# Conformer convolution stage on one core: TensorE convolves a feature tile behind the next tile's projection, and the shifted copy that it reads is made in two parts

## The chip, the cores and the metric

The kernel runs on one core of a Trainium2 chip. The metric is the device time of one execution in microseconds (us); lower is better. A core has TensorE (PE, matrix products into PSUM; PEld are its weight loads), VectorE (DVE), ScalarE (ACT), GpSimd (POOL), and SyncE (SP), which issues nearly all DMA transfers of this kernel. Each engine works through its own list of instructions in order; semaphores tie the lists together.

## What is computed

One inference step of an encoder with two layers, for 512 frames of a new stream and 16 frames each of 8 running streams: 640 frames of 1024 features. Layer 0 is a convolution module and an FFN, layer 1 attends to shared keys and values and has an FFN too. The change lies in the convolution module, which is:

```python
def conv_module(h, hist, g, w_pw1, b_pw1, w_dw, b_dw, ln_g, ln_b, w_pw2, b_pw2):
    a, gate = jnp.split(rms_norm(h, g) @ w_pw1 + b_pw1, 2, axis=-1)
    glu = a * jax.nn.sigmoid(gate)
    full = jnp.concatenate([hist, glu], axis=1)        # 30 earlier frames in front
    y = depthwise_conv(full, w_dw) + b_dw              # width 31, each feature by itself
    y = jax.nn.silu(layer_norm(y, ln_g, ln_b))         # mean and variance over the 1024 features
    return h + y @ w_pw2 + b_pw2, full[:, -30:]
```

Everything is float32. A dense product is done as three products of float32r halves (weight high by input high, weight low by input high, weight high by input low), so one output tile of 128 features by 320 frames with 1024 inputs takes 8 x 3 = 24 matmuls.

## The kernel before

Features lie on partitions: the 1024 features are 8 tiles of 128, called c0 to c7 here. The 640 frames are two halves g = 0 and 1 of 320 columns; half 0 holds the 128 sample frames and the first 192 prompt frames, half 1 the other 320 prompt frames.

The module is a list of steps, the string `PLAN`, which `step` works off one by one. Within what the steps issue, a scheduler then sets the order on each engine from priorities and its own timing (`high_priority` blocks are moved ahead); so the order that stands in the program is read off the built program. The steps:

- `a`, `b`, `c`: the projection of a tile, `glu`. It makes four PSUM tiles (two halves of frames, each with a value and a gate; 24 matmuls each), one after the other. ACT reads each out (L563 the tanh of the gate, L566 the value), DVE multiplies them into the buffer `gall` (L570 the sample frames, L576 the prompt frames). The weights of a tile come with `wsplit`: a DMA into `raw`, ACT makes the high half `whi` (L139), DVE the low half `wlo` (L143). All three have two buffers. PSUM has four buffers of the tag `mm`, which projections and convolutions share.
- `d`: the convolution of a tile on DVE (`conv`, L604: 31 multiply-adds per piece, the sum in PSUM). This is how the sample part of c0 to c3 and the prompt part of c1 and c2 are done.
- `q`: the prompt part of c0 and c3 on ACT and POOL (`conv_pool`): ACT makes a product of 512 columns for each tap (L614, tile `cvt`, two buffers), POOL adds it to a sum `ca` (L617). ACT copies the finished sum to `y` (L583).
- `l`, then `S`, `A`, `B`: c4 to c7 on TensorE. `conv_load` has POOL build diagonal weights `w4` (L622) and copies the tile's row of `gall` to DRAM (`sc`, L627); `conv_shift` reads it back in four DMAs, shifted by 0 to 3 frames, into `x4` (L633). `conv_pe` then does 32 matmuls of 32 output rows for each part (L647): `S` the sample frames (128 columns), `A` the prompt frames of half 0 (192), `B` those of half 1 (320). ACT adds the bias and writes `y` (L583).
- `n0`, `n1`: the layer norm of a half (`conv_ln`): `colmean` sums the features by matmuls with a column of constants (L194, three for each tile), after adding the first `LCUT` = 6 tiles up on POOL (L185); `spread` sends a result back to all partitions (L206); squares on ACT (L166); POOL takes the power (L233); DVE multiplies, ACT takes the silu and the high halves.
- `w0`, `w1`: the second projection `pw2` of a half, and after it the FFN.

The string, with `l4 A4 S4 B4` right behind the projection `c4`:

```python
PLAN = ("a0 y a1 x b0 b1 q0 dp1s0 c2 ds1p2 c3 q3 ds2s3 c4 l4 A4 S4 B4 c5 l5 A5 S5 B5 "
        "c6 l6 A6 S6 c7 l7 A7 S7 s0 n0 B6 B7 w0 n1 w1")
```

`x` is the RMS norm of half 1, `s0` writes the convolution history out (`out_convs`, 1472 KB, and `out_convp`).

Of the kernel before, what the change touches and what calls it, by code (L numbers as in the profile page):

```python
# [15 lines left out]
P = 128  # L16
# [31 lines left out]
C01 = 4  # L48
NB1 = 2
SSQ = 'avavavav'  # L50
SCUT = 8
# [17 lines left out]
def tile_trunk(ctx, tc, xT, vecs, hist, w_pw1, w_pw2, w_in0, w_out0, w_in1, w_out1,  # L69
# [9 lines left out]
    uid = [0]  # L79
    gr = list(GS)  # L80
    mm = tps.enter_context(tc.tile_pool(name="mm0", bufs=4, space=PSUM))
    tp = tps.enter_context(tc.tile_pool(name="tp0", bufs=2))
# [80 lines left out]
    def square(s, n, eng="a"):  # L163
        q = tp.tile([P, 384], F32, tag="sq", name=nm("sq"))
# [9 lines left out]

    def colmean(st, pieces, n, cut, tag, eng=nc.gpsimd):
        nt = len(tiles(n))
        srcs = []
        prev = acc = None
        for s in pieces[:cut]:
            if prev is None:  # L180
                prev = s()
                continue
            if acc is None:
                acc = tp.tile([P, 384], F32, tag="acc", name=nm("acc"), bufs=1)
            eng.tensor_tensor(out=acc[:, :n], in0=prev, in1=s(), op=ALU.add)  # L185
            prev = acc[:, :n]
        if prev is not None:
            srcs.append(lambda: prev)
        srcs += pieces[cut:]
        w = len(srcs)  # L190
        for k, f in enumerate(srcs):
            s = f()
            for t, a in enumerate(tiles(n)):
                nc.tensor.matmul(st[:, 512 + t * w + k:513 + t * w + k], s[:, a:a + P],  # L194
                                 onec, start=True, stop=True)
# [24 lines left out]

    def rstd_bc(pieces, n, engs=SQ, cut=CUT, r2=None, eng=nc.gpsimd, newton=False):
        st = w2t()
        nt = len(tiles(n))
        r, v = colmean(st, [lambda s=s, e=e: square(s, n, e) for s, e in zip(pieces, engs)], n,
                       cut, "rst", eng)
        nc.vector.tensor_scalar(out=r[:, :nt], in0=v, scalar1=EPS, scalar2=None,
                                op0=ALU.add)
        if r2 is None:
            r2 = tp.tile([P, 4], F32, tag="rst2", name=nm("rst2"))
        if newton:  # L230
            rsqrt(r2[:, :nt], r[:, :nt])
        else:
            nc.gpsimd.tensor_tensor(out=r2[:, :nt], in0=r[:, :nt], in1=mhalf[:, :nt], op=ALU.pow)  # L233
        return spread(st, r2, n), r2
# [4 lines left out]

    def rms(g, gain, engs=SQ, cut=CUT, eng=nc.gpsimd):  # L240
        n = gr[g][1]
        bc, _ = rstd_bc([hp(g, k) for k in range(KT)], n, engs, cut, None, eng)
        xh, xl = new_xs(g)
        for k in range(KT):
            t = tp.tile([P, 384], F32, tag="n1", name=nm("n1"), bufs=NB1)
            nc.vector.scalar_tensor_tensor(out=t[:, :n], in0=hp(g, k), scalar=col(gain, k),
                                           in1=bc, op0=ALU.mult, op1=ALU.mult)
            xsplit(t[:, :n], xh[:, k, :], xl[:, k, :])
        return xh, xl, None, None

    def rms_late(g, gain, engs=SQ, cut=CUT):
        n = gr[g][1]
        xh, xl = new_xs(g)
        for k in range(KT):
            src = hp(g, k)
            if gain is not None:
                t = tp.tile([P, 384], F32, tag="n1", name=nm("n1"), bufs=NB1)
# [293 lines left out]

    def glu(c, g, wh, wl):
        n = gr[g][1]
        ps = []
        for ab in range(2):
# [3 lines left out]
                xk(xs[g], range(KT)))  # L559
            ps.append(pt[:, :n])  # L560
        with tc.high_priority(offset=HP):
            t = tp.tile([P, 384], F32, tag="t1", name=nm("t1"))
            nc.scalar.activation(out=t[:, :n], in_=ps[1], func=AF.Tanh, scale=0.5,  # L563
                                 bias=hb1[:, KT + c:KT + c + 1])
            a = tp.tile([P, 384], F32, tag="t2", name=nm("t2"))
            nc.scalar.activation(out=a[:, :n], in_=ps[0], func=AF.Identity, scale=0.5,  # L566
# [42 lines left out]
    def conv_pool(c):  # L609
        acc = cp.tile([P, T], F32, tag="ca", name=nm("ca"))  # L610
        for j in range(W):
            wj = dcol(V_DW + c * W + j)
            pr = acc if j == 0 else cp.tile([P, T], F32, tag="cvt", name=nm("cvt"), bufs=2)
            nc.scalar.activation(out=pr, in_=taps(c, 1, j), func=AF.Identity, scale=wj,  # L614
                                 **({} if j else {"bias": col(V_BDW, c)}))
            if j:
                nc.gpsimd.tensor_tensor(out=acc, in0=acc, in1=pr, op=ALU.add)  # L617
        to_y(c, NB * SB, T, acc, func=AF.Copy)

    def conv_load(c):  # L620
        w4 = cp.tile([P, 32, 32], F32, tag="w4", name=nm("w4"), bufs=2)
        nc.gpsimd.tensor_tensor(  # L622
            out=w4, in0=i4[:, None, :].to_broadcast([P, 32, 32]),
            in1=dwv[:, V_DW4 + 32 * c:V_DW4 + 32 * c + 32].unsqueeze(2).to_broadcast([P, 32, 32]),
            op=ALU.mult)
# [4 lines left out]
    def conv_shift(sc, n):  # L630
        x4 = cp.tile([P, 4, NSC + NPC - 4], F32, tag="x4", name=nm("x4"), bufs=2)
# [5 lines left out]
    def conv_pe(c, w4, x4, a, n):  # L637
        pt = mmt()
        for tg in range(8):
            for q in range(4):  # L640
                if a < 0:
                    mv = x4[:, q, 0:NSC].rearrange("p (s w) -> p s w", w=SEG)
                    mv = mv[:, :, 4 * tg:4 * tg + SB]
                else:
                    o = NSC + a + 4 * tg
                    mv = x4[:, q, o:o + n]
                nc.tensor.matmul(pt[32 * q:32 * q + 32, 0:n], w4[:, 4 * tg + q, :], mv,  # L647
                                 start=(tg == 0), stop=(tg == 7))
        to_y(c, 0 if a < 0 else NB * SB + a, n, pt, func=AF.Identity, bias=col(V_BDW, c))

    def conv_ln(g):
        n = gr[g][1]
        mu = w2t()
        order = LNO[g]
        r, v = colmean(mu, [lambda c=c: y[g][:, c, :] for c in order], n, LCUT, "mst")
        if v is not r:
# [7 lines left out]
        for c in range(KT):  # L664
            yc = y[g][:, c, :]
            nc.vector.tensor_tensor(out=yc, in0=yc, in1=bc, op=ALU.mult)
            s = tp.tile([P, 384], F32, tag="n1", name=nm("n1"), bufs=NB1)
            nc.scalar.activation(out=s[:, :n], in_=yc, func=AF.Silu, scale=col(V_LNG, c),
# [4 lines left out]
    def pw2(g, z):  # L673
        n = gr[g][1]
        for m2 in range(KT // 2):
            wh, wl = wsplit(w_pw2[m2], 16, P, pool=PL2[g])
            for i in range(2):
# [10 lines left out]
    def step(op, arg):  # L688
# [5 lines left out]
        elif op == "c":  # L694
            w = wsplit(w_pw1[c], 16, P, pool=PL1[c])
            load_hist(c, c + 1)
# [4 lines left out]
        elif op == "x":  # L701
            xs[1] = rms(1, V_NCONV, SSQ1, 8)
        elif op in "lm":
            w4, sc = conv_load(c)
            x4s[c] = w4, conv_shift(sc, NSC if op == "m" else NSC + NPC - 4)
        elif op == "d":
            conv([(int(arg[i + 1]), int(arg[i] == "p")) for i in range(0, len(arg), 2)])
        elif op == "q":
            conv_pool(c)
        elif op == "S":  # L710
            conv_pe(c, *x4s[c], -1, NB * SB)
        elif op in "pAB":
            a, n = {"p": (0, T), "A": (0, NH - NB * SB), "B": (NH - NB * SB, NH)}[op]
            conv_pe(c, *x4s[c], a, n)
        elif op == "s":
# [12 lines left out]
    hf.close()  # L728
    gr[:] = GR
    tps, early = ExitStack(), ExitStack()  # L730
    op_ = early.enter_context(tc.tile_pool(name="op", bufs=1, reuse_waits="tile"))
# [433 lines left out]
```

## Time and profile before

| | us |
|---|---|
| median of 3 runs | 1636.82 |
| lowest and highest | 1635.42, 1638.98 |
| the profiled execution | 1640.0 |
| its span in the profile | 1638.2 |
| TensorE busy in the span | 1508.8 (92%) |
| start of c5's projection on TensorE, from the span's start | 128.55 |
| first matmul of `pw2`, from the span's start | 277.51 |

A row of a timeline or of the chain gives the start and the length in us, then engine, line, operation, and output <- input; in square brackets stands how long the engine was idle before the row and what ended that. A row of windows gives, for one stretch of time, the busy time of PE, PEld, DVE, ACT and POOL with the number of instructions, the granted TensorE clock as a share of full speed, the DMA share, and GB/s. A row of groups gives all instructions of one kind and shape: number, busy us in total, mean ns of one, then idle time ahead and what ended it. "PE 5956..." in the page is the busy share in tenths in 40 slices of 41 us.

### The profile page before, as it was taken

What the parts mean: (1) busy time and instruction counts of PE and PEld (TensorE: products, weight loads), DVE (VectorE), ACT (ScalarE), POOL (GpSimd) and SP (SyncE); (2) the same over time, 40 slices, a digit from 0 to 9 for tenths busy, and PEclk for the clock granted to TensorE, in tenths of its full rate; (3) what the DMA queues carried; (4) which work ended last, traced back from release to release, by engine and by line L of the source; (5) the groups of instructions that cost most, each with busy time, mean ns of one, the idle gap of its engine ahead of it and who ended that gap; (6) DMA issues with size and microseconds to landing.
All of it is one profiled execution on the core that took longest, in us unless ns stands there. A gap on an engine that the chain in (4) does not pass through costs nothing.

```text
span 1638.2 us, 27200 instructions
## 1 busy us (share of the span) xinstructions
PE 1508.8 (92%) x11156; PEld 1435.8 (88%) x11156; DVE 996.3 (61%) x1990; ACT 675.5 (41%) x1295; POOL 244.6 (15%) x259
## 2 busy tenths in 40 slices
PE   5956659999999999999899899997899999999997
PEld 5955558989999999999898689895899999999997
DVE  5798003479557557556566656765486565566655
ACT  3565114445424325334555435453344244244243
POOL 5588200410000000001422211110100000000001
PEclk9977776999999999999999999999899999999998
DMA  6243340331222312312445545553012222223211
GB/s 212 71 115 84 83 123 1 103 129 46 84 78 71 110 52 81 100 63 92 139 145 183 174 139 181 171 186 116 26 52 79 102 78 68 87 78 104 78 52 64
DMA packets 52891, 163.99 MB, mean 100 GB/s; under 512 B 9632, under 2 KB 21536, under 8 KB 44064
## 3 DMA queue, kind: packets, MB, share of 16 engines
q1 hardware_dynamic: 52480, 161.96, 30.7%
q8 instruction: 87, 1.43, 0.4%
q10 hardware_dynamic: 288, 0.31, 0.1%
q14 instruction: 36, 0.29, 0.1%
HBM read 150.89 MB, written 11.36 MB: 99 GB/s over the span
## 4 chain that ended last, share of the span: by engine, by line
PE 83%; DVE 5%; POOL 5%; DMA 4%; ACT 2%; issue 2%; SPq 0%; POOLq 0%; DVEq 0%; ACTq 0%
PE mm L352 34%; PE mm L159 13%; PE mm L160 13%; PE mm L161 13%; POOL ca L617 4%; PE mm L647 2%; DMA x<-sc 2%; PE w L194 1%; PE am L947 1%; PE w L962 1%; PE am L993 1%; DMA cache<-in_ck 1%; PE am L930 1%; ACT whi L139 1%; PE w L206 1%
## 5 line engine op out<-in xcount | busy, mean ns | idle before, releaser
L352 PE MATMUL mm<-XH,wlo 128*128 128x320 f32 x736 | 228.8, 311 | 1.1 <-DVE wlo L310 1.1
L352 PE MATMUL mm<-XH,whi 128*128 128x320 f32 x736 | 227.3, 311 | 0.0
L352 PE MATMUL mm<-XL,whi 128*128 128x320 f32 x736 | 225.3, 309 | 0.0
L159 PE MATMUL mm<-xh,whi 128*128 128x320 f32 (+2 forms) x640 | 203.4, 320 | 5.0 <-ACT xh L148 4.5
L160 PE MATMUL mm<-xh,wlo 128*128 128x320 f32 (+2 forms) x640 | 202.3, 317 | 0.0
L161 PE MATMUL mm<-xl,whi 128*128 128x320 f32 (+2 forms) x640 | 197.5, 315 | 0.0
L160 PE MATMUL mm<-hid,wlo 128*128 128x320 f32 (+2 forms) x560 | 171.8, 308 | 0.0
L161 PE MATMUL mm<-hid,whi 128*128 128x320 f32 (+2 forms) x560 | 169.7, 308 | 0.0
L159 PE MATMUL mm<-hid,whi 128*128 128x320 f32 (+2 forms) x560 | 167.7, 308 | 0.0
L309 ACT ACTIVATE whi<-raw 128x1536 fp32r<-128x1536 f32 (+2 forms) x90 | 100.9, 1148 | 122.7 <-PE mm L161 90.6
L310 DVE TENSOR_TENSOR wlo<-raw,whi 128x1536 fp32r<-128x1536 f32 (+2 forms) x90 | 118.6, 1341 | 39.0 <-ACT whi L309 38.8
L352 PEld LDWEIGHTS mm<-XH,wlo 128*128 128x128 f32 x736 | 139.0, 189 | 2.2 <-DVE wlo L310 2.2
L352 PEld LDWEIGHTS mm<-XH,whi 128*128 128x128 f32 x736 | 138.6, 189 | 0.0
L352 PEld LDWEIGHTS mm<-XL,whi 128*128 128x128 f32 x736 | 137.8, 188 | 0.0
L159 PEld LDWEIGHTS mm<-xh,whi 128*128 128x128 f32 x640 | 124.1, 194 | 7.6 <-ACT xh L148 5.3
L160 PEld LDWEIGHTS mm<-xh,wlo 128*128 128x128 f32 x640 | 124.4, 195 | 1.1 <-issue 0.8
L161 PEld LDWEIGHTS mm<-xl,whi 128*128 128x128 f32 x640 | 121.9, 192 | 1.6 <-issue 1.4
L352 PE MATMUL mm<-XH,vhi 128*128 128x320 f32 x368 | 114.2, 310 | 0.3 <-ACT XH L436 0.3
L352 PE MATMUL mm<-XL,vhi 128*128 128x320 f32 x368 | 113.7, 310 | 0.9 <-DVE XL L437 0.8
L352 PE MATMUL mm<-XH,vlo 128*128 128x320 f32 x368 | 114.0, 310 | 0.0
L160 PEld LDWEIGHTS mm<-hid,wlo 128*128 128x128 f32 x560 | 105.1, 188 | 0.0
L161 PEld LDWEIGHTS mm<-hid,whi 128*128 128x128 f32 x560 | 104.7, 188 | 0.0
(201 smaller groups left out, 3442.4 us busy)
## 6 DMA issues: line engine op xcount, KB each, us to landing
raw<-in_w_in SPq DMA_DIRECT2D x38, 1024.0 KB
cache<-in_ck SPq DMA_DIRECT2D x32, 512.0 KB
cache<-in_cv SPq DMA_DIRECT2D x32, 512.0 KB
raw<-in_w_pw SPq DMA_DIRECT2D x14, 1024.0 KB
raw<-in_w_out SPq DMA_DIRECT2D x18, 768.0 KB
raw<-in_w_kq SPq DMA_DIRECT2D x8, 1024.0 KB
x<-sc SPq DMA_DIRECT2D x16, 454.0 KB
raw<-in_w_in SPq DMA_DIRECT2D x12, 512.0 KB
```

The source lines that it names most:

```text
L139: nc.scalar.activation(out=hi[:, a:b], in_=raw[:, a:b], func=AF.Copy)
L159: nc.tensor.matmul(ps, wh, xh, start=(i == 0), stop=False)
L160: nc.tensor.matmul(ps, wl, xh, start=False, stop=False)
L161: nc.tensor.matmul(ps, wh, xl, start=False, stop=(i == last))
L194: nc.tensor.matmul(st[:, 512 + t * w + k:513 + t * w + k], s[:, a:a + P], onec, start=True, stop=True)
L206: nc.tensor.matmul(st[:, a:a + P], r[:, t:t + 1].to_broadcast([P, P]), ident, start=True, stop=True)
L309: nc.scalar.activation(out=hi[:, a:b], in_=src, func=AF.Copy)
L310: nc.vector.tensor_tensor(out=lo[:, a:b], in0=src, in1=hi[:, a:b].bitcast(F32), op=ALU.subtract)
L352: nc.tensor.matmul(pt, wt, v[x][:, k, :], start=(first and k == i == 0), stop=(k == 3 and i == 2), skip_group_check=True)
L617: nc.gpsimd.tensor_tensor(out=acc, in0=acc, in1=pr, op=ALU.add)
L647: nc.tensor.matmul(pt[32 * q:32 * q + 32, 0:n], w4[:, 4 * tg + q, :], mv, start=(tg == 0), stop=(tg == 7))
L930: nc.tensor.transpose(tr[:, o:o + P], S[:, SOFF[i] + k * P:SOFF[i] + (k + 1) * P], ident)
```

## The change

- In `PLAN` a tile's convolution on TensorE comes after the next tile's projection: `C4 ... C5 S4 A4 B4 C6 S5 A5 C7 s0 S6 A6 S7 A7 n0 B5 L7 B6 B7`. The three halves `B5`, `B6`, `B7` now all stand behind `n0`, where `B6` and `B7` stood.
- The step `C` issues a projection and, between its two halves, the copy of what half 0 gives (`xa`, 590 columns: sample frames and `A`); after half 1 the copy for `B` (`xb`, 350 columns). Each copy is one DMA to DRAM and four back. For c7 the read of `xb` is issued by the step `L7`, behind `B5`. The weights `w4` are built ahead, with three buffers instead of two.
- `wsplit` for the next tile is called ahead of a tile's projection, and the first weights of `pw2` ahead of c7's.
- `cvt` has four buffers instead of two (`CVT`).
- `x1` puts the RMS norm of half 1 between the two PSUM tiles of c1's half 0; three of its scratch tiles use the `w4` buffers.
- The mean of `n0` sends all 8 tiles through TensorE (`LCUT if g else 0`): 24 matmuls of one column instead of 9.
- Scratch tiles are 320 columns wide in this stage, not 384, and the last group of taps uses 96 partitions instead of 128.

```diff
-PLAN = ("a0 y a1 x b0 b1 q0 dp1s0 c2 ds1p2 c3 q3 ds2s3 c4 l4 A4 S4 B4 c5 l5 A5 S5 B5 c6 l6 A6 S6 c7 l7 A7 S7 s0 n0 B6 B7 w0 n1 w1")
+PLAN = ("a0 y x1 b0 b1 q0 dp1s0 c2 ds1p2 c3 C4 q3 ds2s3 C5 S4 A4 B4 C6 S5 A5 C7 s0 S6 A6 S7 A7 n0 B5 L7 B6 "
+        "B7 w0 n1 w1")
...
-            pr = acc if j == 0 else cp.tile([P, T], F32, tag="cvt", name=nm("cvt"), bufs=2)
+            pr = acc if j == 0 else cp.tile([P, T], F32, tag="cvt", name=nm("cvt"), bufs=CVT)
...
-        sc = dr.tile([P, NSC + NPC], F32, tag="sc", name=nm("sc"), bufs=2)
-        nc.sync.dma_start(sc, gall[:, c, :])
-        return w4, sc
+        return w4
+
+    def conv_shift(c, tag, c0, n, late=False):
+        nt = NXA if tag == "a" else NXB
+        sc = dr.tile([P, nt], F32, tag="s" + tag, name=nm("s" + tag), bufs=3)[:, 0:n]
+        nc.sync.dma_start(sc, gall[:, c, c0:c0 + n])
+        return (lambda: conv_read(sc, tag, n, nt)) if late else conv_read(sc, tag, n, nt)
+
+    def conv_read(sc, tag, n, nt):
+        x4 = cp.tile([P, 4, nt], F32, tag="x" + tag, name=nm("x" + tag), bufs=2)
         for s in range(4):
-            nc.sync.dma_start(x4[32 * s:32 * s + 32, :, 0:n],
-                              sc[:, s:s + n].rearrange("(q p) w -> p q w", q=4))
+            nc.sync.dma_start(x4[32 * s:32 * s + 32, :, 0:n - s],
+                              sc[:, s:n].rearrange("(q p) w -> p q w", q=4))
         return x4
...
-        r, v = colmean(mu, [lambda c=c: y[g][:, c, :] for c in order], n, LCUT, "mst")
+        r, v = colmean(mu, [lambda c=c: y[g][:, c, :] for c in order], n, LCUT if g else 0, "mst")
...
-            xs[1] = rms(1, V_NCONV, SSQ1, 8)
-        elif op in "lm":
-            w4, sc = conv_load(c)
-            x4s[c] = w4, conv_shift(sc, NSC if op == "m" else NSC + NPC - 4)
+            def mid():
+                xs[1] = rms(1, V_NCONV, SSQ1, 8, hold=w4t)
+            glu(1, 0, *pws[1], mid=mid)
+        elif op in "DC":
+            load_hist(c, c + 1)
+            w4 = conv_load(c)
+            pws[c + 1] = wsplit(w_pw1[c + 1] if c + 1 < KT else w_pw2[0], 16, P)
+            glu(c, 0, *pws[c])
+            xa = conv_shift(c, "a", 0, NXA if op == "C" else NSC)
+            glu(c, 1, *pws[c])
+            x4s[c] = w4, xa, op == "C" and conv_shift(c, "b", NSC + HA, NXB, c == KT - 1)
```

How this moves instructions shows at three places. The first is TensorE around c4's convolution. Before, it stands right behind c4's own projection (whose weights are `whi_155`, `wlo_156`) and ahead of c5's (`whi_172`):

```order
L161 MATMUL mm_162_1211<-xl_50_359,whi_155_1124 128x320
L647 MATMUL mm_168_1250<-x4_167_1245,w4_165_1241 32x192 x32
L647 MATMUL mm_169_1284<-x4_167_1245,w4_165_1241 32x128 x32
L647 MATMUL mm_170_1318<-x4_167_1245,w4_165_1241 32x320 x32
L159 MATMUL mm_174_1359<-xh_16_154,whi_172_1353 128x320
```

Now it stands behind the projection of c5, whose weights are `whi_127` and `wlo_128` in the changed program, and ahead of c6's (`whi_175`):

```order
L165 MATMUL mm_184_1360<-xh_46_327,wlo_128_975 128x320
L166 MATMUL mm_184_1360<-xl_47_328,whi_127_974 128x320
L668 MATMUL mm_189_1397<-xa_134_1037,w4_125_971 32x128 x32
L668 MATMUL mm_190_1431<-xa_134_1037,w4_125_971 32x192 x32
L668 MATMUL mm_191_1465<-xb_140_1099,w4_125_971 32x320 x32
L164 MATMUL mm_196_1508<-xh_16_154,whi_175_1267 128x320
```

So one whole projection lies between the copy of c4 and its use, and the first two parts read `xa`, the third `xb`.

The second place is ACT in c7's projection. Before, the four reads of PSUM (L566, L563) follow each other, and c3's sum `ca` was copied away long ago:

```order
L566 ACTIVATE t2_210_1835<-mm_207_1783,hb1_87 128x320
L563 ACTIVATE t1_209_1833<-mm_208_1808,hb1_87 128x320
L566 ACTIVATE t2_214_1891<-mm_211_1839,hb1_87 128x320
L563 ACTIVATE t1_213_1889<-mm_212_1864,hb1_87 128x320
L139 ACTIVATE whi_252_2222<-raw_251_2221 128x2048
```

Now the two copies of c3's sum `ca_141`, which wait for POOL's last addition, stand between the first and the second read (`t1_216` is the gate of half 0):

```order
L579 ACTIVATE t2_217_1762<-mm_214_1710,hb1_87 128x320
L596 ACTIVATE y0_102<-ca_141_1104 128x192
L596 ACTIVATE y1_103<-ca_141_1104 128x320
L576 ACTIVATE t1_216_1760<-mm_215_1735,hb1_87 128x320
L579 ACTIVATE t2_223_1825<-mm_220_1773,hb1_87 128x320
L576 ACTIVATE t1_222_1823<-mm_221_1798,hb1_87 128x320
```

The third place is SP at c7's copy. Before, the history goes out first (it waits for the sample frames of half 0 only), then c7's copy, which waits for the whole projection:

```order
L716 DMA out_convs<-gall_95 1024x1x368
L627 DMA sc_216_1896<-gall_95 128x912
L717 DMA out_convp<-gall_95 1024x1x30
L633 DMA x4_217_1898<-sc_216_1896 32x4x908 x4
```

Now `out_convs` and c7's first copy `sa_218` wait for the same half and stand one behind the other, and the read for `B7` comes last:

```order
L748 DMA out_convs<-gall_95 1024x1x368
L644 DMA sa_218_1766<-gall_95 128x590
L650 DMA xa_219_1768<-sa_218_1766 32x4x590
L650 DMA xa_219_1768<-sa_218_1766 32x4x589
L650 DMA xa_219_1768<-sa_218_1766 32x4x588
L650 DMA xa_219_1768<-sa_218_1766 32x4x587
L644 DMA sb_224_1828<-gall_95 128x350
L749 DMA out_convp<-gall_95 1024x1x30
L133 DMA raw_268_2375<-in_w_pw2 128x2048
L650 DMA xb_253_2132<-sb_224_1828 32x4x350
```

More of the change, by code (lines that the diff above doesn't have):

```diff
@@ L49 @@
 NB1 = 2
+CVT = 4
+HA = T + NB * SB - 320 - NB * SB
+NXA, NXB = NB * SEG + HIST + HA, HIST + 320
 SSQ = 'avavavav'
@@ L163, in square @@
     def square(s, n, eng="a"):
-        q = tp.tile([P, 384], F32, tag="sq", name=nm("sq"))
+        q = tp.tile([P, tw[0]], F32, tag="sq", name=nm("sq"))
         if eng == "a":
@@ L183, in colmean @@
             if acc is None:
-                acc = tp.tile([P, 384], F32, tag="acc", name=nm("acc"), bufs=1)
+                acc = accp or tp.tile([P, tw[0]], F32, tag="acc", name=nm("acc"), bufs=1)
             eng.tensor_tensor(out=acc[:, :n], in0=prev, in1=s(), op=ALU.add)
@@ L238, in hp, with rms @@
         return h[:, k, g0:g0 + n]
-    def rms(g, gain, engs=SQ, cut=CUT, eng=nc.gpsimd):
+    def rms(g, gain, engs=SQ, cut=CUT, eng=nc.gpsimd, hold=None):
         n = gr[g][1]
-        bc, _ = rstd_bc([hp(g, k) for k in range(KT)], n, engs, cut, None, eng)
+        bc, _ = rstd_bc([hp(g, k) for k in range(KT)], n, engs, cut, None, eng,
+                        accp=hold and hold())
         xh, xl = new_xs(g)
         for k in range(KT):
-            t = tp.tile([P, 384], F32, tag="n1", name=nm("n1"), bufs=NB1)
+            t = hold() if hold and k < 2 else tp.tile([P, tw[0]], F32, tag="n1", name=nm("n1"),
+                                                       bufs=NB1)
             nc.vector.scalar_tensor_tensor(out=t[:, :n], in0=hp(g, k), scalar=col(gain, k),
@@ L550, in tile_trunk, with w4t, glu @@
     nc.scalar.dma_start(dwv, vecs[:, V_N:])
-    def glu(c, g, wh, wl):
+    def w4t():
+        return cp.tile([P, 1024], F32, tag="w4", name=nm("w4"), bufs=3)
+    def glu(c, g, wh, wl, mid=None):
         n = gr[g][1]
@@ L620, in conv_load @@
     def conv_load(c):
-        w4 = cp.tile([P, 32, 32], F32, tag="w4", name=nm("w4"), bufs=2)
+        w4 = w4t().rearrange("p (a b) -> p a b", a=32)
         nc.gpsimd.tensor_tensor(
@@ L729, in tile_trunk @@
     gr[:] = GR
+    tw[0] = 384
     tps, early = ExitStack(), ExitStack()
```

56 lines of the change are left out of this document (33 added, 23 removed).

## The prediction

> **What bounds the kernel now.** I read the page first for where TensorE is not full, then the waits of TensorE in the first 330 us, then the chain of work and the stages of that stretch.
>
> ```profile
> PE   5956659999999999999899899997899999999997
> PEclk9977776999999999999999999999899999999998
> ...
> PE mm L647 <- DMA x<-sc: 64.5, 4, 17.5
> ```
>
> TensorE is full from slice 7 on; it is half empty in slices 3 to 6, the convolution stage. Nearly all of that is one wait, four times: the convolution (L647) waits for the shifted copy, 64.5 us in all. The chain shows what one such wait consists of, and where the stage ends:
>
> ```profile
> 143.20 0.42 ACT t L563
> 143.65 0.49 DVE gall L576
> 144.17 2.49 DMA sc<-gall
> ...
> 147.99 9.75 DMA x<-sc
> 157.87 11.10 PE mm L647 x192
> ...
> 198.72 6.85 PE mm L647 x128
> ...
> 237.43 8.94 PE mm L647 x162
> ...
> 256.80 7.88 PE w L194 x42
> 264.68 1.50 PE w L206 x6
> ...
> 277.51 0.47 PE mm L159
> ```
>
> From the gate's read (143.20) to the convolution (157.87) it is read-out, product, copy to DRAM (2.49) and copy back (about 11, for 4 x 454 KB). By stage, the columns after the window being busy time with counts for PE, PEld, DVE, ACT, POOL, then the granted clock:
>
> ```profile
> 100.60:118.00 17.40, 0.00 (x0) 0.00 (x0) 16.73 (x35) 10.56 (x16) 13.74 (x10) 0.61 0.66 157
> 128.50:142.50 14.00, 14.00 (x99) 13.95 (x96) 11.99 (x34) 8.57 (x17) 13.39 (x10) 1.00 0.00 1
> 157.90:169.00 11.10, 11.10 (x193) 7.28 (x193) 6.34 (x18) 1.85 (x6) 0.42 (x1) 0.79 0.14 55
> 198.70:205.50 6.80, 6.78 (x129) 5.16 (x129) 0.00 (x0) 0.42 (x1) 0.00 (x0) 0.65 0.17 69
> 400.00:600.00 200.00, 200.00 (x1366) 200.00 (x1366) 121.97 (x191) 74.98 (x120) 0.00 (x0) 1.00 0.25 82
> ```
>
> A projection takes TensorE 14.1 us (96 matmuls) at clock 1.00. After a wait of 15 us the convolution runs at 0.79 and 0.65. And beside the empty TensorE of 100 to 118, DVE and POOL work nearly without a pause: they convolve c0 to c3. That work sets how far TensorE can move forward:
>
> ```profile
> L617 POOL TENSOR_TENSOR ca<-ca,cvt 128x512 f32<-128x512 f32 x60 | 87.6, 1460 | 28.0 <-ACT cvt L614 21.9 <-ACT ca L614 2.2
> L604 DVE SCALAR_TENSOR_TENSOR w<-gall,dwv,w 128x512 f32<-128x512 f32 x60 | 43.2, 750 | 0.2
> L604 DVE SCALAR_TENSOR_TENSOR w<-gall,dwv,w 128x128 f32<-128x128 f32 x120 | 39.4, 352 | 1.8
> L143 DVE TENSOR_TENSOR wlo<-raw,whi 128x2048 fp32r<-128x2048 f32 x6 | 13.7, 2287 | 1.7 <-ACT whi L139 1.6
> ...
> 56.87 3.78 POOL L617 TENSOR_TENSOR ca<-ca,cvt 128x512 f32<-128x512 f32 x2 [17.54 <-ACT cvt L614]
> 106.60 3.13 POOL L617 TENSOR_TENSOR ca<-ca,cvt 128x512 f32<-128x512 f32 x1 [0.90 <-ACT cvt L614]
> 111.94 17.53 POOL L617 TENSOR_TENSOR ca<-ca,cvt 128x512 f32<-128x512 f32 x13 [2.22 <-ACT ca L614]
> 129.44 1.91 POOL L622 TENSOR_TENSOR w<-i,dwv 128x1024 f32<-128x1024 f32 x1
> 151.68 6.63 POOL L617 TENSOR_TENSOR ca<-ca,cvt 128x512 f32<-128x512 f32 x5
> ```
>
> POOL's 60 additions run from 56.87 to 158.31, DVE's convolutions end about then. Before, c7's projection (205 to 220) has nothing to do with them; after, it does.
>
> **The change part by part.** I follow TensorE from the end of c4's projection (100.57, where the first long wait begins) to the first matmul of `pw2` (277.51): 176.9 us.
>
> *RMS norm between two tiles of c1.* Before, TensorE goes from the statistics (L194) by way of POOL's power to the spread (L206):
>
> ```profile
> 37.62 0.58 PE w L194 x6
> 38.46 0.88 POOL rst L233
> 39.38 1.49 PE w L206 x6
> ```
>
> It is idle from 38.2 to 39.4; now 18 matmuls of the other tile (18/96 of 14.1 = 2.6) lie there: 1.2 off. DVE makes four input tiles ahead of the first low half instead of two, which can take some of it back, at most the 1.2; I keep the gain, since 8 matmuls need the high halves alone. c4's projection ends at 99.4.
>
> *Convolutions without the wait, c4 to c6.* The convolution parts split by ACT's reads:
>
> ```profile
> 162.98 0.42 ACT L583 ACTIVATE y<-mm,vec 128x192 f32<-128x192 f32 x1 [3.91 <-PE mm L647]
> 164.72 0.37 ACT L583 ACTIVATE y<-mm,vec 128x128 f32<-128x128 f32 x1 [1.33 <-PE mm L647]
> 169.03 0.53 ACT L583 ACTIVATE y<-mm,vec 128x320 f32<-128x320 f32 x1 [3.60 <-PE mm L647]
> ```
>
> `S` takes 1.75 us, `B` 4.3. `A` took 5.1 right after the wait; without it I scale `S` by 192/128: 2.6 (between 2.6 and 5.1; TensorE comes from a full projection, so the low end). The copy back is bounded by 11 us for 454 KB pieces; the new ones are 590 and 350 columns of 908. For c4, c5 and c6 the `xa` copy starts in the middle of a projection and is used a projection later: 7 + 14.1 us of cover for about 11. Hidden. `B4` follows `A4` and `xb` has 14.1 + 4.4: hidden. So: c5 99.4 + 14.1 = 113.5; S4 A4 B4 8.7: 122.2; c6 136.3; S5 A5 4.4: 140.7; c7 without waits 154.8; S6 A6 4.4.
>
> *What is late next: c7's copy.* S7 and A7 stand behind S6 A6 only, so the 4.4 us and 1.5 us of means are all that covers c7's second half and copy. c7's half 0 is read by `t1_216`, and ahead of that on ACT stand two copies of `ca_141`, which wait for POOL's last addition. POOL: start 56.87 - 1.2 = 55.7; 60 additions 87.6; 60 gaps of 0.07 (17.53 for 13 less 13 x 1.28) 4.2; `w4` of c7 1.9; three sums of 0.86 for the layer norm 2.6; and between the two tiles ACT's list (two copies, a product, a read, a weight half, the first product of c3) 4.5: in all 100.8, so 156.5. The rows for these:
>
> ```profile
> L185 POOL TENSOR_TENSOR acc<-acc,y 128x320 f32<-128x320 f32 x8 | 6.9, 862 | 0.4
> ...
> 103.53 0.51 ACT L563 ACTIVATE t<-mm,hb 128x320 f32<-128x320 f32 x1
> 103.94 1.90 ACT L139 ACTIVATE whi<-raw 128x2048 fp32r<-128x2048 f32 x1
> 109.76 0.72 ACT L583 ACTIVATE y<-ca 128x192 f32<-128x192 f32 x2 [2.69 <-POOL ca L617]
> ...
> 111.00 0.80 ACT L614 ACTIVATE ca<-gall,vec,dwv 128x512 f32<-128x512 f32 x1
> ```
>
> The four buffers take out the waits for ACT that the before row shows (21.9 in all, 17.5 of it ahead of the first addition), not the additions. TensorE has c7's half 0 by 147.8, so ACT is held by some 9 us: copies and read end at 157.8 instead of 148.8, DVE writes `gall` by 158.4. Other reads of PSUM queue behind these on ACT: TensorE waits about 1 us for a buffer at c7 and 1 at A6, inside the wait below.
>
> Then SP: `out_convs`, of the same data, goes first, and it shares the queue:
>
> ```profile
> 213.78 0.66 SPq L716 DMA_DIRECT2D out_convs<-gall  x1
> ...
> GB/s 0 0 0 338 388 369 382 386 366 4 0 0 0 346 346 152 30 0 48 75 124 102 199 194 312 210 204 221 231 205 206 210 218 226 194 376 388 340 36 0
> ```
>
> (Slices of 0.675 us from 213.) The history moves from 215.0 to 219.1, 4 us; c7's first copy queues behind it. 158.4 + 1.0 (two issues) + 4 + 2.1 (295 KB; 456 KB took 2.49) = 165.5; copy back 1.75 + 9.3 x 590/908 = 7.8: 173.3. TensorE stands there from about 161.7 (154.8 + 4.4 + 1.5 + 1): a new wait of some 11.6 us, in place of 17.0. Its bounds: 2 (POOL in no one's way, the copies running beside each other) and 17 as before. S7 A7 then run after a wait again: 6.85. A7 ends at 180.2.
>
> *Layer norm of half 0.* Before, 237.43 + 6.85 = 244.3 to 277.5: 33.2 us with B6 and B7 in it. Now three `B` (12.9), 40 + 9 column matmuls at 7.88/42 = 0.19 (9.2; 15 of them new, 2.9), three spreads (3 x 1.2, 3.5) and a tail of one DVE and two ACT instructions of 320 columns (1.7, an estimate from 0.4 to 0.6 each): 27.3 if TensorE is the bound there; 33.2 if the squares are. I take 27.3, since `B` now lies between the squares. `xb` for B7 needs 1.75 + 3.6 us after B5; B6's first half and 12 column matmuls cover 6.5: hidden. First matmul of `pw2`: 207.5, against 277.5. The 18 squares' matmuls of half 1 that came ahead of it now come behind it, mostly where it waits for ACT: I add 1 (0 to 3.4).
>
> *At no cost:* weights loaded a tile earlier (the buffers are still two, so ACT's half starts when it did); 96 partitions in the last taps; the `w4` builds, in POOL's idle time before 55 (17.54 in the row above); narrower scratch. Their cover gone, POOL's 3 x 1.9 us would go on its chain.
>
> Sum: 277.5 - 207.5 - 1 = 69 off. The profiled execution is 1640.0: 1571. Against the median of 1636.82, 3 lower: 1568.
>
> *A rule against it.* The row at 106.60 is an addition that took 3.13, beside a weight split on DVE, where its neighbours took 1.28 to 1.31. The Trainium skill, SBUF — State Buffer, section "SBUF: two separate sides", says that DVE and GpSimd share one pair of ports under an exclusive lock, taken by a DVE instruction with two SBUF inputs against a GpSimd one that reads SBUF. By that rule the split is such an instruction and the trace agrees (3.13); the convolutions on DVE, whose sum is in PSUM, are not, and the trace agrees there too (13 additions in 17.53). Six splits instead of five then fall into POOL's run: 1.6 us more than I count. The same skill, TensorE: Matmul & The Clock Gate, section "What's actually happening", halves the clock after an idle window of about 3.4 us; by it S7 A7 take 4.4 instead of 6.85 if the new wait is shorter than that.
>
> **Rivals.** All times against the median.
>
> *A: as above*, c7's copy late behind POOL and the history: 1568. For it: the POOL sum has no slack, and the order on ACT and SP.
>
> *B: POOL keeps up*, so `t1_216` is done at 148.8 and everything behind it is 9 earlier: 1559. For it: POOL's end is a sum of small terms; it needs additions of 1.31 throughout (60 x 0.15 = 9 less).
>
> *C: the product waits hold ACT further, and ACT's late reads hold PSUM.* ACT then reads c6 and c7 late by more than three tiles' time, TensorE waits for buffers, and the layer norm stays at 33.2: POOL 6 later and 6 in the norm, 1580. For it: DVE has 96 us of convolutions (43.2 + 39.4) and splits (13.7) with less idle time, and it is in order too. Against: four buffers are 5.5 us of slack.
>
> *D: the change doesn't do what it says for one or two tiles:* SP's copies stand behind a weight load that waits, and two of the waits of 15 us stay: 1598. Against: each weight load ahead of a copy waits for a split that is done a projection earlier.
>
> *E: slower.* Every addition on POOL becomes as slow as the one at 106.60: 60 x (3.13 - 1.46) = 100 later: 1668. It decides from 69/60 = 1.15 us more for each addition. The 13 additions in 17.53 beside a busy DVE speak against.
>
> **How the numbers follow.** A 0.48, B 0.20, C 0.24, D 0.05, E 0.03. The time is A's: 1568. The range holds A, B and C with the bounds of the new wait (2 to 17 instead of 11.6, so -10 and +5) and of the layer norm (+6): 1554 to 1588; D and E stay outside. A change of under 0.2% (3 us) can't be told from none here; A to D are all faster by more: 0.96, same 0.01, slower 0.03.
>
> **What would show it.** In the changed profile: no wait of L668 for `xa` at c4, c5 and c6, and one of 9 to 14 us at S7; granted clock near 1.00 in S4 to A6; ACT's `t1` of c7 waiting for POOL's `ca`, POOL's last addition at 154 to 158; `pw2` beginning near 207 and everything behind it as before. I am wrong if S7 doesn't wait (B, or the copies run beside each other), if TensorE waits for ACT in c6 or c7 by more than 2 us (C), or if waits for `xa` stand at c4 to c6 (D).

## The result: 56 us faster, with a norm and a start of `pw2` that cost 14 more than predicted

| | before | predicted | changed |
|---|---|---|---|
| median, us | 1637.90 (4 runs, 1635.42 to 1640.09) | 1568 (1554 to 1588) | 1581.91 (4 runs, 1578.88 to 1585.53) |
| ratio to before, 95% interval | | | 0.9659 [0.963, 0.9689] |

In a later series the ratio was 0.9656 [0.964, 0.9672]. The profiled execution took 1584.37 with a span of 1582.6, against 1638.2 before: 55.6 less. TensorE's share and the clock in 40 slices, from the page of the changed kernel:

```profile
PE   5999798999999999999899899997999999999997
PEclk9999778999999999999999999998899999999998
```

Of the slices that were half empty, 3 to 6, one is still thin: 5, with 7 in it, and further back slice 7 has 8. The waits of TensorE in the first 330 us (total, number, longest):

```profile
PE w L199 <- DVE acc L190: 13.0, 1, 13.0
PE mm L668 <- DMA xa<-sa: 10.8, 1, 10.8
...
PE w L211 <- POOL rst L239: 4.8, 2, 3.2
```

The 13.0 is the start of the program, before the first matmul. The convolution waits for its copy once, 10.8 us, where it waited four times, 64.5 us in all. The chain shows where that one comes from, and what stands in the way behind it:

```profile
147.57 3.23 POOL ca L630
159.25 6.24 DMA sa<-gall
166.87 6.56 DMA xa<-sa
173.67 5.75 PE mm L668 x112
180.86 3.71 PE w L199 x32
...
207.01 2.78 PE w L199 x18
...
216.02 3.63 PE w L199 x18
...
254.33 3.38 POOL wlo L148
```

POOL's additions, then c7's copy behind the history, then column matmuls (L199), and at the end a weight split on POOL. The same by stage, as windows (busy time with counts of PE, PEld, DVE, ACT, POOL, then the granted clock): the convolutions S4 and A4, S5 and A5, S6 and A6, then S7 A7, the layer norm, `pw2` on half 0 in three pieces:

```profile
109.80:114.30 4.50, 4.50 (x133) 3.93 (x136) 4.50 (x11) 2.75 (x5) 4.19 (x4) 1.00 0.97 275
134.50:140.10 5.60, 4.77 (x128) 3.73 (x128) 2.88 (x8) 4.33 (x9) 5.36 (x6) 1.00 0.15 54
155.60:160.60 5.00, 4.38 (x125) 3.67 (x128) 3.15 (x10) 3.60 (x6) 1.37 (x2) 1.00 0.41 160
173.60:180.90 7.30, 6.65 (x129) 5.59 (x130) 0.00 (x0) 0.70 (x3) 0.00 (x0) 0.73 0.46 133
180.90:213.50 32.60, 31.66 (x308) 21.49 (x308) 6.42 (x20) 8.63 (x17) 2.58 (x3) 0.87 0.10 24
213.50:228.60 15.10, 15.08 (x61) 15.08 (x62) 8.10 (x19) 8.83 (x19) 0.00 (x0) 0.50 0.00 1
228.60:252.20 23.60, 23.60 (x165) 23.60 (x163) 7.45 (x10) 6.10 (x4) 10.35 (x3) 1.00 0.31 94
252.20:262.50 10.30, 3.77 (x25) 3.30 (x23) 6.04 (x10) 3.85 (x6) 4.23 (x2) 0.69 0.51 192
```

The three pieces of `pw2` on half 0 before:

```profile
277.50:285.20 7.70, 7.70 (x32) 7.70 (x32) 3.35 (x8) 6.58 (x14) 0.00 (x0) 0.50 0.00 0
285.20:310.10 24.90, 24.90 (x171) 24.90 (x171) 7.45 (x10) 5.74 (x3) 10.35 (x3) 1.00 0.28 89
310.10:316.50 6.40, 2.85 (x18) 2.47 (x16) 4.23 (x10) 3.49 (x5) 3.95 (x2) 0.70 0.39 151
```

Put side by side, in us from the span's start:

| | before | predicted | changed |
|---|---|---|---|
| end of c5's projection | 142.9 | 113.5 | 109.8 |
| POOL's last addition ends | 158.3 | 156.5 | 157.0 |
| TensorE stands for c7's copy | 220.4 to 237.4 | 161.7 to 173.3 | 162.9 to 173.7 |
| end of A7 | 244.3 | 180.2 | 180.9 |
| first matmul of `pw2`, half 0 | 277.5 | 207.5 | 213.5 |
| first matmul of `pw2`, half 1 | 316.5 | 247.5 | 262.5 |
| end of the span | 1638.2 | 1569.2 | 1582.6 |

Up to the end of A7 the forecast is off by 0.7. The layer norm adds 5.3 to that, `pw2` on half 0 another 9.0, and everything behind gives 1.6 back: 13.4 in all. That the forecast is so close at A7 is luck in part: c5's projection ends 3.7 early, and from there to the wait TensorE needs 53.1 us (109.8 to 162.9) instead of 48.2 (113.5 to 161.7).

### The profile page after: what moved, and what is told of

The parts are those of the page before. It is cut to its first block, busy times and chain, and to the rows that moved or that the text cites. A ratio compares the mean times of both kernels' runs of the same rounds, so it can differ in the third digit from the quotient of the medians.

```text
span 1582.6 us, 27281 instructions
## 1 busy us (share of the span) xinstructions
PE 1502.5 (95%) x11186; PEld 1429.4 (90%) x11186; DVE 1001.3 (63%) x1990; ACT 674.4 (43%) x1295; POOL 240.7 (15%) x253
## 4 chain that ended last, share of the span: by engine, by line
PE 85%; POOL 6%; DVE 3%; DMA 2%; ACT 2%; issue 1%; POOLq 0%; SPq 0%; DVEq 0%; ACTq 0%
PE mm L360 35%; PE mm L164 13%; PE mm L166 13%; PE mm L165 13%; POOL ca L630 5%; PE w L199 1%; PE mm L668 1%; PE w L995 1%; PE am L980 1%; PE am L963 1%; PE am L1026 1%; DMA cache<-in_ck 1%; ACT whi L144 1%; PE w L939 1%; PE w L211 1%
## 5 line engine op out<-in xcount | busy, mean ns | idle before, releaser
L360 PE MATMUL mm<-XL,whi 128*128 128x320 f32 x736 | 225.2, 309 | 0.0
L165 PE MATMUL mm<-hid,wlo 128*128 128x320 f32 (+2 forms) x560 | 171.8, 308 | 0.0
```

The source lines that it names most:

```text
L165: nc.tensor.matmul(ps, wl, xh, start=False, stop=False)
L360: nc.tensor.matmul(pt, wt, v[x][:, k, :], start=(first and k == i == 0), stop=(k == 3 and i == 2), skip_group_check=True)
```

## Experiments

Every kernel is the changed one with one edit, or a sum of edits, and was timed against the kernel before. They ran in three series on three chips, so the ratios compare better than the medians. The two profiles of the changed kernel itself differ by 1.4 us in the wait at S7, by 1.2 at the start of `pw2` on half 0 and by 3.0 on half 1; smaller differences between places in the table mean nothing. A wait and the places are in us, from the span's start.

| kernel | median | ratio [95% interval] | wait at S7 | its end | `pw2` half 0 | half 1 |
|---|---|---|---|---|---|---|
| changed, once more | 1584.56 | 0.9656 [0.964, 0.9672] | 12.2 | 173.9 | 212.3 | 259.5 |
| move undone | 1603.22 | 0.9769 [0.9739, 0.9799] | 7.8 | 193.0 | 234.6 | 278.9 |
| 16 taps for c3 | 1573.64 | 0.9596 [0.9566, 0.9626] | 9.3 | 167.1 | 205.5 | 251.6 |
| two product buffers | 1577.56 | 0.9624 [0.9595, 0.9653] | 12.1 | 171.8 | 210.2 | 256.3 |
| history, 7 tiles early | 1586.14 | 0.967 [0.9625, 0.9715] | 12.9 | 172.9 | 217.4 | 264.1 |
| history, 4 tiles early | 1585.39 | 0.9666 [0.9644, 0.9688] | 10.4 | 170.1 | 213.3 | 259.5 |
| old mean | 1583.68 | 0.9641 [0.9625, 0.9657] | 13.2 | 172.3 | 213.8 | 258.8 |
| squares of half 1 on POOL | 1573.52 | 0.9587 [0.9562, 0.9611] | 12.2 | 173.8 | 212.2 | 251.4 |
| squares of both halves on POOL | 1581.49 | 0.9645 [0.9621, 0.9669] | 10.5 | 172.5 | 207.2 | 261.0 |

The baseline of the last series:

> The changed kernel once more, as the baseline for the three others on the same chip: 1580 to 1585, wait of 10 to 12 us at S7.

### The move alone undone

```diff
-C5 S4 A4 B4 C6 S5 A5 C7 s0 S6 A6 S7 A7 n0
+S4 A4 B4 C5 S5 A5 C6 S6 A6 C7 s0 S7 A7 n0
```

> The changed kernel with each tile's convolution right behind its own projection again (S4 A4 B4 ahead of C5, S5 A5 ahead of C6, S6 A6 ahead of C7); copy in two parts, buffers, norm and mean stay as changed. If the later place in the list is what pays: S4, S5 and S6 wait about 5 us each for xa (copy about 11 of which 7 are covered by the projection's second half), each convolution starts at the low clock (1.5 to 2.4 us more), and S7 still waits 5 to 9: 15 to 22 us slower than the changed kernel, about 1600. Rival, that the copy in two parts alone hides the copy: no wait over 2 us at S4 to S6 and 1582.

Measured: 1603.22, 19 above the changed kernel's 1584.56. The wait for the copy in this kernel:

```profile
PE mm L668 <- DMA xa<-sa: 26.3, 4, 10.7
```

The four waits are 10.7, 5.2, 2.7 and 7.8, and the granted clock in the convolutions behind them is 0.57 to 0.77. So the place in the list is worth about 19 of the 56 us. The other 37 come with the rest of the change. Most of it is less waiting: even right behind its own projection a convolution waits 26.3 in all instead of 64.5. That the copy in two parts brings this is likely but not shown, as no run undoes it alone. Why S4 waits 10.7 and S6 only 2.7 was not followed up.

### What holds c7's copy: POOL, ACT's order, DVE, the queue

Sixteen taps instead of 31 for c3's prompt part, so that POOL has 15 additions less:

```diff
-        for j in range(W):
+        for j in range(W if c == 0 else 16):
```

> The changed kernel with 16 instead of 31 taps in c3's prompt part on ACT and POOL (15 products and 15 additions left out). If POOL's last addition holds ACT's read of c7's half 0: POOL ends about 20 us earlier, that read no longer waits for it, c7's copy starts 9 us earlier, S7 waits about 2 us and the time falls by 9 to 1573. Rival, c7's copy is late by itself (its own length and the history): the wait at S7 stays within 2 us of 10.8, 1582.

The time fell by about the 9 expected, but the wait only to 9.3, where 2 was expected. TensorE came 5 us earlier to S7; 3.2 of that are waits in c6 and c7 that are gone, 2.4 of them for ACT's reads. The copy landed 6.6 earlier (167.1 against 173.7), not 9. The next one in line was DVE. Its timeline in this kernel:

```profile
144.12 6.08 DVE L617 SCALAR_TENSOR_TENSOR w<-gall,dwv,w 128x128 f32<-128x128 f32 x16
...
151.28 0.28 DVE L583 SCALAR_TENSOR_TENSOR gall<-t,t 128x128 f32<-128x128 f32 x1
```

ACT had c7's half 0 read out by 147.3, and DVE had convolution pieces ahead of the product (L583) until 151.3. So POOL did hold the copy, and behind it, 3 to 4 us apart, DVE's own list did.

Two product buffers instead of four:

```diff
-CVT = 4
+CVT = 2
```

> The changed kernel with two product buffers instead of four. If POOL's last addition sets c7's copy: the waits of POOL for ACT come back (4.4 us of the 21.9 before lay behind the first addition), POOL ends about 161 instead of 157, the wait at S7 grows from 10.8 to about 15, 1586. Rival, POOL isn't what c7's copy waits for: POOL ends later and the wait at S7 stays at 10.8, 1582.

It went the other way: 1577.56, where 1586 was expected and the changed kernel has 1581.91 and 1584.56. The intervals of the ratios overlap, so a gain is likely, but not shown. POOL's additions in the changed kernel, and then in this one:

```profile
L630 POOL TENSOR_TENSOR ca<-ca,cvt 128x512 f32<-128x512 f32 x60 | 91.5, 1525 | 16.6 <-ACT cvt L627 8.0 <-ACT ca L627 4.4
```

```profile
L630 POOL TENSOR_TENSOR ca<-ca,cvt 128x512 f32<-128x512 f32 x60 | 91.5, 1525 | 18.8 <-ACT cvt L627 12.8 <-ACT ca L627 2.2
```

The waits for products do grow by 4.8, but those for the first product of a sum shrink by 2.2; POOL's idle time grows by 2.2 in all, and it ends 1 us later only, at 158.0. What decides is ACT's order. In the changed kernel, ACT around c7's read:

```profile
157.00 0.72 ACT L596 ACTIVATE y<-ca 128x192 f32<-128x192 f32 x2 [4.01 <-POOL ca L630]
157.63 0.51 ACT L576 ACTIVATE t<-mm,hb 128x320 f32<-128x320 f32 x1
```

and with two buffers:

```profile
154.44 0.51 ACT L576 ACTIVATE t<-mm,hb 128x320 f32<-128x320 f32 x1
155.15 0.72 ACT L627 ACTIVATE cvt<-gall,dwv 128x512 f32<-128x512 f32 x1 [0.21 <-POOL ca L630]
...
158.07 0.72 ACT L596 ACTIVATE y<-ca 128x192 f32<-128x192 f32 x2 [1.78 <-POOL ca L630]
```

With four buffers ACT runs ahead, and the scheduler puts the wait for the whole sum ahead of the gate's read; with two, the products keep pace with POOL and the read stands among them, 3.2 us earlier (2.0 against the second profile of the changed kernel, where it is at 156.5). The copy lands 1.9 and 2.1 earlier, 171.8 against 173.7 and 173.9. The deeper buffer did not pay here; it brought the order that holds c7.

The history earlier, first tiles 0 to 6 ahead of c7's projection, then tiles 0 to 3 during c4's:

```diff
-            nc.sync.dma_start(convs_out, gs)
+                nc.sync.dma_start(convs_out[:, 0:c], gs[:, 0:c])        (first, step s7)
...
+                nc.sync.dma_start(convs_out[:, 7:8], gs[:, 7:8])        (first, step s0)
...
+            nc.sync.dma_start(convs_out[:, a:b], gs[:, a:b])        (second)
...
-A5 C7 s0 S6
+A5 s7 C7 s0 S6        (first)
+q3 s03 ds2s3 ... A5 C7 s47 S6        (second)
```

> The changed kernel with the conv history written in two transfers: tiles 0 to 6 (1288 KB) ahead of c7's projection, tile 7 (184 KB) where all of it was. If the history ahead of c7's copy costs what its transfer takes: sa of c7 lands 3.5 us earlier, the wait at S7 falls from 10.8 to about 7.3, and the time by 3.5 to 1578. Rival, that the transfer only changes its place (c6's copy then waits behind it and S6 stands for it): S6 waits 2 to 3.5 us, 1582.

> The changed kernel with the history of tiles 0 to 3 (736 KB) written during c4's projection and that of tiles 4 to 7 where all of it was. The history of tiles 0 to 6 right ahead of c6's copy gained nothing, since the next weights were then pushed in front of c7's copy. If that was the reason: sa of c7 lands 2 us earlier, the wait at S7 falls from 10.8 to about 8.8, 1580 beside 1582. Rival, c7's copy is not held by the history at all: wait 10.8 and no change.

Neither moved the time. SP's queue around c7's copy, first in the changed kernel, then with seven tiles early, then with four:

```profile
158.50 0.67 SPq L748 DMA_DIRECT2D out_convs<-gall  x1
159.25 0.60 SPq L644 DMA_DIRECT2D sa<-gall  x1
165.56 1.75 SPq L650 DMA_DIRECT2D xa<-sa  x4
```

```profile
155.44 0.38 SPq L133 DMA_DIRECT2D raw<-in_w_pw  x1
...
157.99 0.71 SPq L644 DMA_DIRECT2D sa<-gall  x1
164.93 1.74 SPq L650 DMA_DIRECT2D xa<-sa  x4
```

```profile
157.66 0.46 SPq L644 DMA_DIRECT2D sa<-gall  x1
162.08 1.74 SPq L650 DMA_DIRECT2D xa<-sa  x4
```

From issue to the read back `sa` takes 6.3, 6.9 and 4.4 us. In the nine other profiles with all of the history in front (the changed kernel's second among them) it takes 6.8 to 7.8, and in the other kernel with four tiles early (the first under "A faster version") 4.5. So half of the history less in front saves the copy 2 to 3 us. With seven tiles early, c6's copy comes later, and the weights (1024 KB) are issued at 155.4 instead of 151.5; they seem to stand in the same place as the history did. With four tiles early the copy is 2 us quicker, as expected, and lands at 170.1. But the 24 column matmuls of the mean, eight of which stood ahead of the wait in the changed kernel, now all follow A7, and the clock is 0.50 from 182.5 to 189.0: `pw2` begins at 213.3 all the same. A gain on the queue was given back by TensorE's order.

### What makes the norm and the start of `pw2` long

The old mean for half 0:

```diff
-LCUT if g else 0, "mst")
+LCUT, "mst")
```

> The changed kernel with the old mean for half 0 (six tiles added up on POOL, then 9 column matmuls; the 24 of the changed kernel undone). If TensorE is the bound in the layer norm, it becomes shorter by the 15 column matmuls (0.25 us each at full clock: 3.7, of which a third stood inside the wait at S7): pw2 begins about 2.5 us earlier; the squares of half 1 then fall partly to the end of pw2's first half, which gives 2 to 3 back: within 2 us of the changed kernel. Rival, the mean on TensorE is worth its place: the sums on POOL stand behind its product sums and its weight split, the mean comes late, pw2 begins 3 us later or more, 1585 or slower.

1583.68, no difference. `pw2` begins at 213.8 because twelve of the squares' records of half 1 now come ahead of it. The 24 matmuls of the mean cost nothing that the 9 and POOL's sums do not.

The squares of half 1 added up on POOL, so that one column matmul per 128 frames remains of eight:

```diff
-        bc, _ = rstd_bc([y[g][:, c, :] for c in order], n, SQ, 1)
+        bc, _ = rstd_bc([y[g][:, c, :] for c in order], n, SQ, 8 if g else 1)
```

> The changed kernel with the squares of half 1 added up on POOL (7 additions, one column matmul of three tiles) instead of 24 column matmuls on TensorE. If these column matmuls, spread over the start of pw2, are what makes its first half long (they keep the granted clock at 0.50 from 213 to 228 us and take 8 us themselves, and the last of them stand behind pw2's matmuls, where the spread waits for them): full clock about 4 us after pw2's start, no wait of 3.2 us at the last spread, and the stretch from the first matmul of pw2 half 0 to that of half 1 falls from 49.0 to about 38: 10 us faster, 1572. Rival, POOL's own weight split ahead of its power and the tail behind it set that stretch: 46 or more, 1579 or slower, since POOL gets 6 us more work.

1573.52. `pw2` on half 0 takes 39.3 (212.2 to 251.4) instead of 49.0 and 47.3 in the two profiles of the changed kernel. The clock is back 11 us after its start, where it was 15 in the changed kernel and 4 were expected: TensorE now waits 2.8 in that stretch for the low halves of the input, which DVE makes. Its windows (the first begins 2.3 ahead of A7's end):

```profile
178.50:212.10 33.60, 32.69 (x360) 22.00 (x352) 6.39 (x20) 8.59 (x17) 2.58 (x3) 0.91 0.10 23
212.10:223.30 11.20, 8.38 (x30) 7.98 (x31) 8.69 (x18) 7.36 (x19) 6.33 (x7) 0.50 0.00 0
223.30:247.00 23.70, 23.70 (x165) 23.70 (x164) 9.47 (x14) 7.65 (x7) 11.08 (x4) 1.00 0.27 90
247.00:251.40 4.40, 1.61 (x13) 1.42 (x11) 3.30 (x8) 3.37 (x5) 1.38 (x1) 1.00 0.68 238
```

The tail behind the last `pw2` matmul falls from 10.3 to 4.4. So these 24 column matmuls cost 8 to 11 us, and POOL's seven additions fit beside `pw2`.

Both halves on POOL (`8 if g else 1` becomes `8`):

> As before, with the squares of half 0 on POOL too. If TensorE is the bound in the layer norm of half 0 (33.2 us, of which 24 column matmuls take 6): from the end of A7 to pw2 27 to 29 us, and 4 to 6 us faster than with half 1 alone, about 1567. Rival, the squares are the bound there (ACT makes two, waits until they are consumed): POOL's chain of 7 additions at 0.87 us takes the matmuls' place, the stretch stays at 33, and the time is that of half 1 alone, 1572.

The norm became what was expected, 26.6 us from A7 to `pw2` (180.5 to 207.2), but the time did not. One of the waits of this kernel's TensorE:

```profile
PE w L199 <- POOL acc L190: 10.5, 1, 10.5
```

The scheduler had put one column matmul of half 1's mean behind all of `pw2` on half 0; the subtractions, squares and sums of half 1 waited for it, and TensorE for them.

### A faster version

Two product buffers, the squares of both halves on POOL, and the history in two halves, together:

> Two product buffers, the squares of both halves on POOL, and the history in two halves, together. If the three act in different places (ACT's order ahead of c7's copy, the layer norm and the start of pw2, the queue): 4 + 15 + 2 = 21 us less than the changed kernel, about 1561. If a later stage takes the gain back (POOL's chain, or the squares): 1568 to 1575.

1581.01 (0.963 [0.9605, 0.9654]): the same wait of 10.5 us takes it back, as in the kernel before it. Two ways around it, both without the split history:

```diff
-B7 w0 n1 w1
+B7 n1 w0 w1        (squares of half 1 alone on POOL)
```

> Two product buffers, the squares of half 1 on POOL, and n1 ahead of w0 in the list, so that the last spread of half 1 stands in the middle of pw2's first half instead of behind it. If the gains of the two product buffers (about 5) and of the squares on POOL (10) add, and the wait of 2.8 us and the spread ahead of pw2's second half go: 1560 to 1566. If DVE's multiplications of half 1 come ahead of half 0's and hold pw2 back instead: 1570 to 1575.

1568.11 (0.9555 [0.9537, 0.9574]). And the statistics of half 1 at high priority, with the squares of both halves on POOL:

```diff
+        with tc.high_priority(offset=HP * g):
             r, v = colmean(mu, [lambda c=c: y[g][:, c, :] for c in order], n, LCUT if g else 0, "mst")
...
+        with tc.high_priority(offset=HP * g):
+            bc, _ = rstd_bc([y[g][:, c, :] for c in order], n, SQ, 8)
```

> Two product buffers, the squares of both halves on POOL, and the statistics of half 1 at high priority, so that none of its mean's column matmuls is left behind pw2's matmuls (one of them was, and the wait of 10.5 us for POOL's sum with it). If that one matmul caused the wait: no wait over 2 us between pw2's halves other than the spread's 2.2, half 0's layer norm at 27 us, 1562. If POOL's sums are late anyway: a wait of 5 to 10 us stays, 1572 to 1580.

1566.98 (0.9551 [0.953, 0.9571]), 17.6 below the changed kernel in the same series; 5 above what was expected, and not to be told apart from the 1568.11. Its norm and `pw2` on half 0:

```profile
178.00:203.60 25.60, 21.65 (x266) 12.86 (x257) 5.85 (x17) 8.18 (x17) 10.67 (x13) 1.00 0.12 30
203.60:243.60 40.00, 37.14 (x228) 36.95 (x228) 20.99 (x41) 18.44 (x30) 19.03 (x13) 0.87 0.24 79
```

The first window begins 0.8 ahead of A7's end: the norm takes 24.8 us, at clock 1.00. The wait of 10.5 us is gone; the one at S7 is still 12.2.

## Why the prediction was right, and where it was off

**The moved convolutions (right).** S4 to A6 run at clock 1.00 without a wait for `xa`, and putting them back costs about 19 us.

**The new wait (right).** Forecast 11.6, measured 10.8; the copy landed at 173.7 against 173.3. POOL's end, 156.5 forecast and 157.0 measured, has two errors that cancel: it began at 52.6 and not at 55.7, and an addition took 1.525 and not 1.46 us on average (60 x 0.065 = 3.9). That POOL was behind it is shown by the kernel with 16 taps, though rival B's price of 9 is not: its copy came 6.6 earlier, because DVE's list is next. The four buffers, which I let take out waits, were no help.

**From c5 to S7 (mis-sized, against).** From the end of c5's projection to the wait TensorE took 53.1 and not 48.2. It is busy for 49.8 of it, and idle for 3.3: 2.4 of that in waits for ACT's reads, where I had counted 1 ahead of S7, and 0.8 ahead of S5 with no releaser in the trace.

**The first 100 us (mis-sized, in favour).** c5's projection ended 3.7 earlier than forecast. The norm in c1 gave 2.7 instead of 1.2: TensorE's stretch from its first projection to the end of c4's went from 79.5 to 76.8. I counted the idle time of 1.2 and not the clock, whose mean over that stretch (the column ahead of the last two) was 0.96 before and 1.00 now:

```profile
21.10:100.57 79.47, 77.11 (x492) 0.96 0.24 80
```

```profile
18.85:95.60 76.75, 74.69 (x492) 1.00 0.28 89
```

The other 2.3 come from an edit that I costed at nothing, the `w4` builds (below, in the last section).

**The layer norm (wrong: the term of 27.3).** It took 32.6, and 31.3 in the second profile. I took 49 column matmuls at 0.19 from the row of 42. Those rows count two records for each of these matmuls: the trace has 114 records for 57 matmuls, 98 of them in this stretch. 98 x 0.125 (1.50 for 12) is 12.3, and not 9.2. The `B` parts took 16.3 and not 12.9; they ran partly at the low clock, and the granted clock of the stretch was 0.87. TensorE was the bound, as I had assumed (31.66 busy of 32.60), and not the squares, which rival C had for the same 33.2; with 21 of the column matmuls taken off TensorE, and the 9 of half 1's mean and one spread now behind the start of `pw2`, the norm takes 26.6.

**The half's squares moved behind `pw2`'s start (wrong: the term of +1).** It was 10. By the windows above, the stretch at the low clock is 15.1 us instead of 7.7 (7.4 more), the one at full clock 23.6 instead of 24.9 (1.3 less), and the tail 10.3 instead of 6.4 (3.9 more). The 24 column matmuls lie across the first 12 us of `pw2` and at its end. They take 8.0 us of `pw2` themselves, against 2.7 before, when 15 of them came ahead of it. The clock stays at 0.50 among them, and the last of them stand in the tail, with the split on POOL ahead of the power. I gave them 0 to 3.4 as mere busy time. Taking them off gave 8 to 11 us back.

**Behind it (right).** From the first matmul of half 1 on, 1320.1 against 1321.7.

So the time came out near rival C's 1580 without most of its mechanism. Its sign was there, just: TensorE's waits for ACT's reads in c6 and c7 were 2.4 in all, and more than 2 was to mean C. But POOL was on time, not 6 late, and the norm was long for another reason. What was lost against 1568 was lost behind A7. The bounds that I gave for A's own terms (5 for the wait, 6 for the norm) end at 1579; that 1581.91 lies inside the range comes from the room that it has for the rivals, and is luck as far as A goes.

## What to carry over

Once a long wait is gone, the time is set by what the moved work now stands next to: look at the next stage's order and clock, not only at the stage that was changed. Before a count from a program is multiplied by a duration from a trace, check with one group that both count the same thing. A deeper buffer lets an engine run ahead, and so can let a scheduler put a long wait in front of an urgent read; the order shows that before any run does.

## What the hardware did that I had not expected

**The clock falls during column matmuls as if TensorE were idle.** In the changed kernel TensorE has no gap over 1.0 us between 206 and 252 us. Its granted clock, window by window:

```profile
206.00:214.00 8.00, 7.04 (x46) 0.64 0.00 1
...
224.00:228.00 4.00, 4.00 (x18) 0.50 0.00 0
228.00:230.00 2.00, 2.00 (x13) 0.82 0.00 0
```

It falls to 0.50 at 208.2, during 2.8 us of matmuls that are one column wide (206.9 to 209.7), stays there through 15 us of busy time with more of them in it, and comes back 3.5 us after their last group (225.2 to 228.7). The start of the norm shows the same: from 180.9 to 184.3 TensorE does nothing but column matmuls, busy all the time, and from 184.3 to 187.7 its clock is 0.51. In the second profile of the same kernel no fall follows that group, so such a group can bring the clock down but need not. The Trainium skill, TensorE: Matmul & The Clock Gate, section "What's actually happening", has the clock fall after an idle window of about 3.4 us and return after as long a busy one. The return agrees with the 3.5 measured here. The fall comes without an idle window; it would fit if such matmuls are not counted as busy, or not fully. No run here separates the two.

**POOL and DVE stop each other, both ways.** The prediction shows an addition on POOL held up beside a split on DVE (3.13 us). Here DVE is held up beside POOL. At the start, DVE's squares before, beside POOL's two `w4` builds (5.89 to 10.07 us), and then in the changed kernel, which builds them later:

```profile
6.23 2.08 DVE L169 TENSOR_TENSOR sq<-h 128x320 f32<-128x320 f32 x1
8.23 3.31 DVE L185 TENSOR_TENSOR acc<-acc,sq 128x320 f32<-128x320 f32 x3
```

```profile
7.03 0.49 DVE L174 TENSOR_TENSOR sq<-h 128x320 f32<-128x320 f32 x1
7.53 1.02 DVE L190 TENSOR_TENSOR acc<-acc,sq 128x320 f32<-128x320 f32 x2
```

A square took 2.08 instead of 0.49, and TensorE's first matmul came at 15.2 instead of 13.0. It is in 12.3 to 13.0 in all profiles of the changed form; of the form before there is one. And at the end of `pw2` on half 0, beside POOL's split of 3.38 from 254.33 on:

```profile
255.75 1.98 DVE L232 TENSOR_SCALAR rst<-rst 128x3 f32<-128x3 f32 x1
```

Before, the same instruction took 0.17, ahead of the split. The Trainium skill, SBUF — State Buffer, section "SBUF: two separate sides", gives whoever comes first the shared ports for its whole instruction. The squares, with two inputs in SBUF, agree (2.08 and 0.49). The last one has a single input, of three columns, and it ends with POOL's split (both at 257.7). By that section such an instruction contends only in a mode that uses both ports, and the `tensor_scalar` that it is can enter one; no run here shows whether this one did.
